# Chunk decays as running sums: a 4-row matmul and an identity matmul spread them, ScalarE's bias subtracts, and VectorE takes GpSimd's elementwise work

## The chip, the cores and the metric

The kernel runs on one core of one Trainium2 chip. The time is the device time of a whole launch in microseconds (us). A core has five instruction streams that work side by side and meet at semaphores: TensorE (PE, matmuls, results into PSUM), VectorE (DVE, elementwise), ScalarE (ACT, `exp`, `ln`, copies with scale and bias), GpSimd (POOL, elementwise from and to SBUF) and SyncE (SP, which issues most DMAs). Each works through its own instructions in the order in which they were laid down. An instruction at the head of a stream that waits holds back everything behind it there, whatever that is for.

## The reference

One encoder layer over 1,280 tokens (one sequence of 1,024, one of 256), 1,024 wide, in fp32: a projection into many columns, three mixers side by side (gated delta rule, retention, windowed attention), an output projection, a gated second input and a final norm. The change touches the gated delta rule's preparation, for chunks of 64 tokens, 6 heads and two directions:

```python
decay = jnp.cumsum(to_chunks(g, CHUNK), axis=-1)
incl = idx[:, None] >= idx[None, :]
gamma = jnp.exp(jnp.where(incl, decay[..., :, None] - decay[..., None, :], -jnp.inf))
a_mat = jnp.einsum('nbhcd,nbhsd->nbhcs', k_beta, k) * gamma
qk    = jnp.einsum('nbhcd,nbhsd->nbhcs', q, k) * gamma
q_dec = q * jnp.exp(decay)[..., None]
k_dec = k * jnp.exp(decay[..., -1:] - decay)[..., None]
```

`gamma` is a 64 x 64 matrix for each chunk and head: `exp` of the difference of two running sums of the gate `g` on one side of the diagonal, zero on the other. `t_mat`, the unit lower triangle of `a_mat`, is then inverted.

## The kernel before, in words

**Products.** Activations and weights are split in two fp32r parts (`xh`, `xl`; `whi`, `wlo`), and a product is a sum of three matmuls (`dense`, tile `mm`; two PSUM buffers of each tag). `load_w` fetches 128 columns of weights by SP, makes `whi` on ACT and `wlo` = raw - whi on POOL. In the gate products ACT evacuates (`evg`, tile `sz`, one buffer), three more ACT operations make the sigmoid in `sg`, POOL multiplies the two, and SP writes the result to DRAM.

**Convolutions.** Nine products feed a 5-tap convolution: four `scalar_tensor_tensor` of 128 x 1284 each on DVE (L522). Six of the nine (queries and keys) are normalised: ACT makes `rr`, POOL multiplies into `kq` (L544).

**Preparation** (`prep_stream`). It runs over ten blocks b of 128 tokens, from 9 down to 0, and in each over the two directions d, so 20 steps; PE's instructions of 11 products (`PP`) are spread between them. A step: DVE forms `gt` (128 x 768), the gates `ghl` (two fp32r parts) times a 0/1 triangle `MR`; two PE matmuls with `LA`, of which the one half sums and the other masks, turn it into decay differences in two PSUM tiles `sb`; ACT takes four `exp` of 64 x 384 into `ge` (L597); DVE multiplies `ge[:, 0]` by the triangle again to zero what lies beyond the diagonal (tile `ge`, L600). Then DVE multiplies Gram matrices (`sa`, in PSUM) and keys (`kc`) by `ge` into `at` and `l2`, POOL multiplies queries by `ge[:, 1]` into the rest of `l2` (L613), and SP writes `at` and `l2` to DRAM (`agd`, `ad`, `l2d`).

**Inversion** (`invert(g)`, group g=1 after block 5, g=0 after block 0). It reads `agd` back into `ot` and does some sixty dependent DVE operations of 120 rows; the result goes out as `yd`. The scan of the chunks (`join`, `step`) reads `yd` and runs beside attention and retention; the output projection follows.

**What sets the order.** `weave` and `spread` lay the work of the streams down by planned lengths, and the scheduler orders each engine's instructions from a simulated timeline; on the chip that order is fixed. Pool buffers decide how far one engine may run ahead of another: `sb`, `sa`, `tr` and `mm` have two PSUM buffers, `ge` and `l2` two, `gt`, `kc`, `at` and `sz` one.

Of the kernel before, what the change touches and what calls it, by code (L numbers as in the profile page):

```python
# [52 lines left out]
def encoder_kernel(ctx: ExitStack, tc: tile.TileContext, I, O, dbg=None, upto=99):  # L53
# [33 lines left out]
    def tt(eng, out, a, b, op):  # L87
        eng.tensor_tensor(out=out, in0=a, in1=b, op=op)  # L88
# [161 lines left out]
    for i in range(2):  # L250
        S.copy(LA[:, :, i, 64 - 64 * i:128 - 64 * i], bc(ones[:, 0:64].unsqueeze(1), [128, 2, 64]))
    for d in range(2):
        sg = 1 if d == 0 else -1
        t = tmpp.tile([128, 128], F32, name=f"mltmp{d}")
        sel(t, onesbd, ALU.is_gt, 0.0, 0, sg, [[-sg, 128]])
        tt(V, t[:, 0:64], t[:, 0:64], t[:, 64:128], ADD)
        for i in range(2):
            S.copy(LA[:, d, i, 64 * i:64 * i + 64], t[:, 0:64])
        t2 = pt_([128, 128], f"mrbd{d}")
        sel(t2, onesbd, ALU.is_ge, 0.0, 0, -sg, [[sg, 128]])  # L260
        MRbd.append(t2)
        m = pt_([128, 64], f"mr{d}")
        tt(V, m, t2[:, 0:64], t2[:, 64:128], ADD)
        MR.append(m)
# [201 lines left out]
    def product(n):  # L466
        if n in GCOL:
            def evg(pp, t0, w):
                o = ot[:, n, t0:t0 + w]
# [2 lines left out]
                S.copy(zt, pp[:, :w])  # L472
# [27 lines left out]
    with tc.tile_pool(name="pa", reuse_waits="tile", bufs=2) as pa:  # L500
# [65 lines left out]
        def prep_stream():  # L566
            for b in reversed(range(NB)):
# [18 lines left out]
                for d in range(2):  # L586
                    gt = pa.tile([128, 2, 6, 64], F32R, tag="gt", name=nm("gt"), bufs=1)
                    tt(V, gt, bc(ghl[:, d, :, 2 * b:2 * b + 2, :].bitcast(F32).rearrange("p l c q -> p l (c q)").unsqueeze(3),
                                 [128, 2, 6, 64]),
                       bc(MR[d].unsqueeze(1).unsqueeze(1), [128, 2, 6, 64]), MUL)  # L590
                    gf = [gt[:, i].rearrange("p q t -> p (q t)") for i in range(2)]
                    ge = pa.tile([128, 2, 2, 3, 64], F32, tag="ge", name=nm("ge"))
                    for i, r in enumerate((T, B)):
                        pd = ps("sb")
                        mm(pd[:, 0:384], LA[:, d, i], gf[i])
                        for w, rw in enumerate((T, B)):
                            S.activation(out=ge[rw, (w + i) % 2].rearrange("p c q t -> p (c q t)"), in_=pd[rw, 0:384], func=AF.Exp)  # L597
# [614 lines left out]
```

## Time and profile before

| what | us |
|---|---|
| median of 3 runs | 1153.72 |
| the runs | 1153.5 to 1154.53 |
| profiled execution | 1150.47 |
| its span (first to last instruction) | 1148.8 |

The mean granted TensorE clock over the span is 0.947 of full speed, and the DMA engines move 105 GB/s on average. In what follows a busy time is the time in which an engine had an instruction under way. A figure in square brackets behind a row of the timeline is how long the engine had been idle before it, and what ended that. A duration contains any time for which the instruction itself was held up after its start.

### The profile page before, as it was taken

The numbers are of one execution on the slowest core, as the hardware profiler recorded it, in microseconds if no ns is written. First come the engines' busy times: TensorE is split into PE (matmuls) and PEld (weight loads), VectorE is DVE, ScalarE is ACT, GpSimd is POOL, SyncE is SP. The second block draws the span as 40 slices with busy tenths as digits, with TensorE's granted clock in tenths as the row PEclk, the third lists the DMA queues.
The fourth block names the chain that finished last, engine by engine and source line by source line (L and its number), as shares of the span: only waits on it lengthen the run. The fifth ranks groups of instructions, "written<-read, shape, count | busy, mean of one in ns | idle before, by whom it ended". The sixth has DMA issues, their size and how long they took to land.

```text
span 1148.8 us, 25993 instructions
## 1 busy us (share of the span) xinstructions
PE 1042.9 (91%) x10345; PEld 959.0 (83%) x10345; DVE 666.8 (58%) x1297; ACT 531.3 (46%) x1208; POOL 426.2 (37%) x494
## 2 busy tenths in 40 slices
PE   6999989978778868799979999999879999999996
PEld 5989989968677867698868888888659999999996
DVE  6667667586899769626774465476856123411125
ACT  8575675666555433424643422323333012455554
POOL 3133333454554534114241434655462111214421
PEclk9999999999979888999988999999758999999998
DMA  7112202448244652435463343546547232101003
GB/s 243 37 43 60 61 19 60 117 144 195 74 126 136 164 136 84 87 77 134 123 148 92 96 116 104 140 116 168 148 138 240 90 102 92 46 2 47 10 37 147
DMA packets 196531, 120.63 MB, mean 105 GB/s; under 512 B 100266, under 2 KB 181338, under 8 KB 196410
## 3 DMA queue, kind: packets, MB, share of 16 engines
q1 hardware_dynamic: 196410, 118.97, 37.8%
q8 instruction: 82, 1.34, 0.5%
q14 instruction: 39, 0.32, 0.1%
HBM read 76.14 MB, written 42.78 MB: 104 GB/s over the span
## 4 chain that ended last, share of the span: by engine, by line
PE 58%; DVE 18%; DMA 9%; ACT 6%; issue 4%; SPq 3%; POOL 1%; DVEq 0%; ACTq 0%; POOLq 0%
PE mm L85 29%; PE sa L85 15%; DVE ot L88 8%; PE sb L85 7%; PE tr L85 3%; DVE ot L522 3%; DMA ad<-at 2%; SPq L616 1%; DMA agd<-at 1%; DVE l L88 1%; DMA ot<-agd 1%; PE tr L842 1%; DMA yd<-ot 1%; PE tr L1154 1%; ACT ge L597 1%
## 5 line engine op out<-in xcount | busy, mean ns | idle before, releaser
L85 PE MATMUL mm<-xh,whi 128*128 128x256 f32 x1200 | 351.5, 293 | 26.4 <-ACT sz L472 13.4
L85 PE MATMUL mm<-xl,whi 128*128 128x256 f32 x1200 | 348.2, 290 | 0.0
L85 PE MATMUL mm<-xh,wlo 128*128 128x256 f32 x1200 | 346.5, 289 | 0.2 <-POOL wlo L88 0.2
L85 PEld LDWEIGHTS mm<-xh,whi 128*128 128x128 f32 x1200 | 233.6, 195 | 34.3 <-ACT sz L472 15.2
L85 PEld LDWEIGHTS mm<-xl,whi 128*128 128x128 f32 x1200 | 233.4, 194 | 3.2 <-issue 1.4
L85 PEld LDWEIGHTS mm<-xh,wlo 128*128 128x128 f32 x1200 | 233.1, 194 | 3.4 <-issue 1.5
L88 POOL TENSOR_TENSOR wlo<-raw,whi 128x1024 fp32r<-128x1024 f32 (+1 forms) x37 | 106.7, 2885 | 207.7 <-ACT whi L1068 104.1
L88 DVE TENSOR_TENSOR ot<-ot 128x1284 f32<-128x1284 f32 (+16 forms) x131 | 115.8, 884 | 43.2 <-DMA ot<-agd 21.0
L85 PE MATMUL mm<-whi,xh 128*128 128x256 f32 x320 | 91.8, 287 | 0.0
L85 PE MATMUL mm<-whi,xl 128*128 128x256 f32 x320 | 91.7, 287 | 0.0
L85 PE MATMUL mm<-wlo,xh 128*128 128x256 f32 x320 | 91.7, 287 | 0.0
L85 PE MATMUL sa<-whi,xh 128*128 128x256 f32 x320 | 91.3, 285 | 0.1
L85 PE MATMUL sa<-whi,xl 128*128 128x256 f32 x320 | 90.8, 284 | 0.0
L85 PE MATMUL sa<-wlo,xh 128*128 128x256 f32 x320 | 90.5, 283 | 0.0
L522 DVE SCALAR_TENSOR_TENSOR ot<-ot,cols 128x1284 f32<-128x1284 f32 x36 | 76.1, 2115 | 23.1 <-ACT ot L517 22.3
L88 DVE TENSOR_TENSOR sgm<-sb,sgm 128x256 f32<-128x256 f32 x40 | 17.0, 424 | 94.7 <-ACT sgm L101 74.2
L88 POOL TENSOR_TENSOR l<-kq,ge 64x384 f32<-64x384 f32 x40 | 48.2, 1204 | 58.5 <-ACT ge L597 45.3
L88 POOL TENSOR_TENSOR ot<-ot,sgm 128x256 f32<-128x256 f32 x40 | 30.4, 761 | 88.9 <-DVE sgm L88 88.7
L85 PEld LDWEIGHTS mm<-whi,xh 128*128 128x128 f32 x320 | 61.8, 193 | 0.0
L85 PEld LDWEIGHTS mm<-whi,xl 128*128 128x128 f32 x320 | 61.6, 193 | 0.0
L85 PEld LDWEIGHTS mm<-wlo,xh 128*128 128x128 f32 x320 | 61.7, 193 | 0.0
L85 PEld LDWEIGHTS sa<-whi,xh 128*128 128x128 f32 x320 | 60.7, 190 | 0.4 <-DVE gt L1027 0.4
(289 smaller groups left out, 2217.2 us busy)
## 6 DMA issues: line engine op xcount, KB each, us to landing
raw<-in_w_in SPq DMA_DIRECT2D x28, 512.0 KB, 3.8
l2d<-l SPq DMA_DIRECT2D x20, 576.0 KB, 4.5
l<-l2d SPq DMA_DIRECT2D x40, 288.0 KB, 2.9
xt<-in_x_prompt SPq DMA_DIRECT2D x8, 512.0 KB, 6.6
x<-in_x_prompt SPq DMA_DIRECT2D x32, 128.0 KB, 2.3
raw<-in_w_pg SPq DMA_DIRECT2D x4, 1024.0 KB
yp<-ot SPq DMA_DIRECT2D x8, 512.0 KB, 2.6
ad<-at SPq DMA_DIRECT2D x20, 198.0 KB, 3.5
```

Of the source, the lines that this page charges most:

```text
L85: nc.tensor.matmul(out, lhsT, rhs, start=start, stop=stop)
L88: eng.tensor_tensor(out=out, in0=a, in1=b, op=op)
L522: V.scalar_tensor_tensor(out=Y[:, 0:1284], in0=R[:, j:j + 1284], scalar=cw(ti, j), in1=Y[:, 0:1284], op0=MUL, op1=ADD)
L597: S.activation(out=ge[rw, (w + i) % 2].rearrange("p c q t -> p (c q t)"), in_=pd[rw, 0:384], func=AF.Exp)
L616: nc.sync.dma_start(out=AGD[d][b // 5][q, 2 * b % 10:2 * b % 10 + 2].rearrange("c p r x -> r (c p) x"), in_=at[32 * q:32 * q + 32, :, :, q ...
L842: nc.tensor.transpose(pt[:, k * 128:(k + 1) * 128], pr[:, k * 128:(k + 1) * 128], ident)
L1154: nc.tensor.transpose(pt[:, k * 128:(k + 1) * 128], hb[:, b, (n * 4 + k) * 128:(n * 4 + k + 1) * 128], ident)
```

## The change

- **Decay.** A matmul `MRbd[d]` against the gates already made running sums (`pd`). Its negative is kept as `negd`. The running sums are also formed transposed (60 chunk-and-head rows), split in two fp32r parts (`dr`) and written to DRAM (`DRD`). Each step reads back four rows of 384 numbers into `dj` by two DMAs from POOL's queue. A matmul with four rows, `SD[i]` (0/1, which picks the half of the chunk pair), spreads them over the 128 partitions, and for i=0 an identity matmul adds a mask `MB` of 0 or -1e30. ACT takes six `exp` of 128 x 64 with `negd` as bias for `ge[:, 0]`, and one of 128 x 384 for `ge[:, 1]`. `gt`, `ghl`, `LA`, `MR` and the second masking are gone.
- **Engines.** `wlo` in `load_w`, the gate product in `evg`, the multiply into `kq` and the multiply of the queries into `l2` go from POOL to VectorE.
- **Buffers.** `sz` has two.

```diff
         with tc.high_priority():
             S.copy(hi, raw)
-            tt(G, lo, raw, hi.bitcast(F32), SUB)
+            tt(V, lo, raw, hi.bitcast(F32), SUB)
...
+    SD = [pt_([4, 128], f"sd{i}", F32R) for i in range(2)]
     for i in range(2):
+        for l in range(2):
+            for h in range(2):
+                nc.gpsimd.dma_start(out=SD[i][2 * l + h:2 * l + h + 1], in_=onesbd[64 * (h ^ i):64 * (h ^ i) + 1])
...
-        for d in range(2):
-            for i in range(2):
-                src = sab[64 * i:64 * i + 64, 1, d]
-                S.copy(ghl[0:64, d, i], src)
-                tt(V, ghl[64:128, d, i], src, ghl[0:64, d, i].bitcast(F32), SUB)
...
+            V.tensor_scalar(out=f(negd[:, d]), in0=pd[:, 0:60], scalar1=-1.0, scalar2=None, op0=MUL)
+            pr = ps("tr")
+            mm(pr[0:60, 0:128], f(sab[:, 1, d]), MRbd[d])
+            dr = pa.tile([60, 2, 128], F32R, tag="kc", name=nm("dr"), bufs=1)
+            S.copy(dr[:, 0], pr[0:60, 0:128])
+            tt(V, dr[:, 1], pr[0:60, 0:128], dr[:, 0].bitcast(F32), SUB)
+            nc.gpsimd.dma_start(out=DRD[d], in_=dr)
...
-                zt = gp.tile([128, 512], F32, tag="sz", name=nm("sz"), bufs=1)[:, :w]
+                zt = gp.tile([128, 512], F32, tag="sz", name=nm("sz"))[:, :w]
                 S.copy(zt, pp[:, :w])
                 sigmoid(sg, zt)
-                tt(G, sg, sg, zt, MUL)
+                tt(V, sg, sg, zt, MUL)
...
-                        tt(G, kq[:, p, 1 if isq else 0, t0 + s0:t0 + s0 + n], Z[:, o + s0:o + s0 + n], rr[:, :n], MUL)
+                        tt(V, kq[:, p, 1 if isq else 0, t0 + s0:t0 + s0 + n], Z[:, o + s0:o + s0 + n], rr[:, :n], MUL)
...
-                    gt = pa.tile([128, 2, 6, 64], F32R, tag="gt", name=nm("gt"), bufs=1)
-                    tt(V, gt, bc(ghl[:, d, :, 2 * b:2 * b + 2, :].bitcast(F32).rearrange("p l c q -> p l (c q)").unsqueeze(3),
-                                 [128, 2, 6, 64]),
-                       bc(MR[d].unsqueeze(1).unsqueeze(1), [128, 2, 6, 64]), MUL)
+                    dj = pa.tile([4, 6, 64], F32R, tag="dj", name=nm("dj"))
+                    for l in range(2):
+                        nc.gpsimd.dma_start(out=dj[2 * l:2 * l + 2], in_=DRD[d][6 * b:6 * b + 6, l].rearrange("n (s t) -> s n t", s=2))
...
-                    for i, r in enumerate((T, B)):
+                    for i in range(2):
                         pd = ps("sb")
-                        mm(pd[:, 0:384], LA[:, d, i], gf[i])
-                        for w, rw in enumerate((T, B)):
-                            S.activation(out=ge[rw, (w + i) % 2].rearrange("p c q t -> p (c q t)"), in_=pd[rw, 0:384], func=AF.Exp)
-                    gm = ge[:, 0].rearrange("p c q t -> p (c q) t")
-                    tt(G if b in MG else V, gm, gm, bc(MR[d].unsqueeze(1), [128, 6, 64]), MUL)
+                        mm(pd[:, 0:384], SD[i], djf, stop=bool(i))
+                        if i == 0:
+                            mm(pd[:, 0:384].rearrange("p (n t) -> p n t", n=6), identR, bc(MB[d].unsqueeze(1), [128, 6, 64]), start=False)
+                            for n in range(6):
+                                S.activation(out=ge[:, 0, n // 3, n % 3], in_=pd[:, 64 * n:64 * n + 64], func=AF.Exp,
+                                             bias=negd[:, d, 2 * b + n // 3, n % 3:n % 3 + 1])
+                        else:
+                            S.activation(out=ge[:, 1].rearrange("p c q t -> p (c q t)"), in_=pd[:, 0:384], func=AF.Exp)
...
-                        tt(G, l2[lr, :, :, h, :], kq[lr, :, 1, tb].rearrange("p q (c t) -> p c q t", c=2), ge[lr, 1], MUL)
+                        tt(V, l2[lr, :, :, h, :], kq[lr, :, 1, tb].rearrange("p q (c t) -> p c q t", c=2), ge[lr, 1], MUL)
```

VectorE's order at the start of the preparation, before (names: `ge`, `gt`, `at`, `l` are a step's tiles, `sa` the Gram matrices, `mr` the triangle, `kc` the keys; the number behind a name tells tiles apart):

```order
L88 TENSOR_TENSOR ge_2170<-ge_2170,mr_334 128x384
L88 TENSOR_TENSOR at_2180<-sa_2145,ge_2170 128x6x32
L88 TENSOR_TENSOR l_184_2181<-sa_2145,ge_2170 64x3x64 x2
L88 TENSOR_TENSOR at_2180<-sa_2152,ge_2170 128x6x32
L88 TENSOR_TENSOR l_184_2181<-sa_2152,ge_2170 64x3x64 x2
L88 TENSOR_TENSOR l_184_2181<-kc_2163,ge_2170 128x6x64
L88 TENSOR_TENSOR gt_2367<-ghl,mr_334 128x768
L88 TENSOR_TENSOR ge_2265<-ge_2265,mr_343 128x384
```

and the same place now:

```order
L88 TENSOR_TENSOR at_2193<-sa_2154,ge_2180 128x6x32
L88 TENSOR_TENSOR l_188_2194<-sa_2154,ge_2180 64x3x64 x2
L88 TENSOR_TENSOR at_2193<-sa_2161,ge_2180 128x6x32
L88 TENSOR_TENSOR l_188_2194<-sa_2161,ge_2180 64x3x64 x2
L88 TENSOR_TENSOR l_188_2194<-kc_2172,ge_2180 128x6x64
L88 TENSOR_TENSOR l_188_2194<-kq,ge_2180 64x6x64 x2
L88 TENSOR_TENSOR wlo_2708<-raw_2705,whi_2707 128x1024
L88 TENSOR_TENSOR at_2292<-sa_2154,ge_2279 128x6x32
```

A step has lost its two triangle multiplies, and POOL's two multiplies of queries and its weight split stand in VectorE's stream.

VectorE's order where the first inversion begins, before (`ot<-ot` rows are the inversion, the first of them waits for `agd` to come back):

```order
L88 TENSOR_TENSOR l_283_3032<-kc_2891,ge_3021 128x6x64
L88 TENSOR_TENSOR ot<-ot 120x2x32x32
L88 TENSOR_TENSOR ot<-ot 120x2x30 x2
L88 TENSOR_TENSOR ot<-ot 120x2x58
L88 TENSOR_TENSOR ot<-ot 120x2x2x29
```

and now (`sg<-sg,sz` are gate products, `wlo` the weights of a product to come):

```order
L88 TENSOR_TENSOR sg_3255<-sg_3255,sz_3256 128x512
L88 TENSOR_TENSOR ot<-ot 120x2x32x32
L88 TENSOR_TENSOR ot<-ot 120x2x30 x2
L88 TENSOR_TENSOR ot<-ot 120x2x58
L88 TENSOR_TENSOR ot<-ot 120x2x2x29
L88 TENSOR_TENSOR ot<-ot 120x2x84
L88 TENSOR_TENSOR ot<-ot 120x2x3x28
L88 TENSOR_TENSOR ot<-ot 120x2x108
L88 TENSOR_TENSOR sg_3330<-sg_3330,sz_3331 128x512
L88 TENSOR_TENSOR ot<-ot 120x2x4x27
L88 TENSOR_TENSOR wlo_3392<-raw_3389,whi_3391 128x1024
```

Gate products and weight splits now stand between and behind the inversion's operations, behind the one that waits for a DMA.

POOL's order in the preparation now (`dj` the four decay rows of a step, `drd` their place in DRAM, `elc` a small copy that stays on POOL):

```order
L373 DMA drd_382<-dr_924 60x256
L594 DMA dj_2276<-drd_382 2x6x64 x2
L594 DMA dj_2384<-drd_381 2x6x64 x2
L525 MEMSET ot 128x4 x5
L621 COPY elc<-ge_2180 128x6
L594 DMA dj_2501<-drd_382 2x6x64 x2
L621 COPY elc<-ge_2279 128x6
```

The `dj` loads of a step stand two steps ahead of the copy that belongs to it.

More of the change, by code (lines that the diff above doesn't have):

```diff
@@ L244, in sel @@
                         pattern=pat, channel_multiplier=cm)
-    MR, MRbd = [], []
-    LA = pt_([128, 2, 2, 128], "la", F32R)
-    for i in range(2):
-        S.copy(LA[:, :, i, 64 - 64 * i:128 - 64 * i], bc(ones[:, 0:64].unsqueeze(1), [128, 2, 64]))
-    for d in range(2):
[L253 to L256, printed above, removed]
-        for i in range(2):
[L258 to L264, printed above, removed]
+    identR = pt_([128, 128], "identR", F32R)
+    S.copy(identR, ident)
+    MRbd, MB = [], []
+    for d in range(2):
+        t2 = ot[:, 7, 256 + 128 * d:384 + 128 * d]
+        sel(t2, onesbd, ALU.is_ge, 0.0, 0, 2 * d - 1, [[1 - 2 * d, 128]])
+        MRbd.append(t2)
+        t = tmpp.tile([128, 64], F32, name=f"mbtmp{d}")
+        tt(V, t, t2[:, 0:64], t2[:, 64:128], ADD)
+        m = pt_([128, 64], f"mb{d}", F32R)
+        V.tensor_scalar(out=m, in0=t, scalar1=-1.0, scalar2=1e30, op0=ADD, op1=MUL)
+        MB.append(m)
+    SD = [pt_([4, 128], f"sd{i}", F32R) for i in range(2)]
+    for i in range(2):
+        for l in range(2):
+            for h in range(2):
+                nc.gpsimd.dma_start(out=SD[i][2 * l + h:2 * l + h + 1], in_=onesbd[64 * (h ^ i):64 * (h ^ i) + 1])
     sumid = pt_([128, 24], "sumid")
@@ L310, in encoder_kernel @@
     sab = ct([128, 2, 2, NC, 3], "sab")
-    ghl = ct([128, 2, 2, NC, 3], "ghl", F32R)
+    negd = ct([128, 2, NC, 3], "negd")
     nbeta = ct([128, 2, NC, 3], "nbeta")
@@ L314, in encoder_kernel, with beta_alpha @@
     elc = ct([128, 2, NC, 3], "elc")
-    def beta_alpha():
+    DRD = [tc.dram_tile([60, 2, 128], F32R, name=f"drd{d}") for d in range(2)]
+    def beta_alpha(pa):
         abT = ot[:, 6, 0:NT]
@@ L355, in beta_alpha @@
                         (V if f else G).tensor_copy(dst[:, f, d, :, par, :], src[:, f, :, d, :, 1 - half])
-        for d in range(2):
-            for i in range(2):
-                src = sab[64 * i:64 * i + 64, 1, d]
-                S.copy(ghl[0:64, d, i], src)
-                tt(V, ghl[64:128, d, i], src, ghl[0:64, d, i].bitcast(F32), SUB)
         V.tensor_scalar(out=nbeta, in0=sab[:, 0], scalar1=-1.0, scalar2=None, op0=MUL)
@@ L509, in encoder_kernel @@
             if i == 2:
-                beta_alpha()
+                beta_alpha(pa)
             R, Y, Z = ot[:, 3 * z, :], ot[:, 3 * z + 1, :], ot[:, 3 * z + 2, :]
@@ L586, in prep_stream @@
                 for d in range(2):
-                    gt = pa.tile([128, 2, 6, 64], F32R, tag="gt", name=nm("gt"), bufs=1)
-                    tt(V, gt, bc(ghl[:, d, :, 2 * b:2 * b + 2, :].bitcast(F32).rearrange("p l c q -> p l (c q)").unsqueeze(3),
-                                 [128, 2, 6, 64]),
-                       bc(MR[d].unsqueeze(1).unsqueeze(1), [128, 2, 6, 64]), MUL)
-                    gf = [gt[:, i].rearrange("p q t -> p (q t)") for i in range(2)]
+                    dj = pa.tile([4, 6, 64], F32R, tag="dj", name=nm("dj"))
+                    for l in range(2):
+                        nc.gpsimd.dma_start(out=dj[2 * l:2 * l + 2], in_=DRD[d][6 * b:6 * b + 6, l].rearrange("n (s t) -> s n t", s=2))
+                    djf = dj.rearrange("r n t -> r (n t)")
                     ge = pa.tile([128, 2, 2, 3, 64], F32, tag="ge", name=nm("ge"))
-                    for i, r in enumerate((T, B)):
+                    for i in range(2):
                         pd = ps("sb")
-                        mm(pd[:, 0:384], LA[:, d, i], gf[i])
-                        for w, rw in enumerate((T, B)):
-                            S.activation(out=ge[rw, (w + i) % 2].rearrange("p c q t -> p (c q t)"), in_=pd[rw, 0:384], func=AF.Exp)
-                    gm = ge[:, 0].rearrange("p c q t -> p (c q) t")
-                    tt(G if b in MG else V, gm, gm, bc(MR[d].unsqueeze(1), [128, 6, 64]), MUL)
+                        mm(pd[:, 0:384], SD[i], djf, stop=bool(i))
[6 more added lines that the diff above has]
+                            S.activation(out=ge[:, 1].rearrange("p c q t -> p (c q t)"), in_=pd[:, 0:384], func=AF.Exp)
                     at = pa.tile([128, 2, 3, 2, 33], F32, tag="at", name=nm("at"), bufs=AB)
@@ L610, in prep_stream @@
                         tt(V, l2[B, r, :, 0, :], g3[r][B, :, 64:128], ge[B, 0, r], MUL)
-                    tt(G if b in KG else V, l2[:, :, :, 2, :], kc, bc(gl, [128, 2, 3, 64]), MUL)
+                    tt(V, l2[:, :, :, 2, :], kc, bc(gl, [128, 2, 3, 64]), MUL)
                     for h, lr in enumerate((T, B)):
-                        tt(G, l2[lr, :, :, h, :], kq[lr, :, 1, tb].rearrange("p q (c t) -> p c q t", c=2), ge[lr, 1], MUL)
+                        tt(V, l2[lr, :, :, h, :], kq[lr, :, 1, tb].rearrange("p q (c t) -> p c q t", c=2), ge[lr, 1], MUL)
                     G.tensor_copy(elc[:, d, 2 * b:2 * b + 2, :], el.rearrange("p c q t -> p c (q t)"))
```

## Prediction

> **What bounds the kernel now.** I read the page's busy table first, then busy time by stage, then the waits, then the timeline around the longest waits.
>
> ```profile
> PE 1042.9 (91%) x10345; PEld 959.0 (83%) x10345; DVE 666.8 (58%) x1297; ACT 531.3 (46%) x1208; POOL 426.2 (37%) x494
> core 0: us, PE busy (x) PEld busy (x) DVE busy (x) ACT busy (x) POOL busy (x), PEclk, DMA share, GB/s
> 9.00:40.00 31.00, 28.10 (x201) 26.15 (x200) 24.51 (x32) 25.26 (x61) 5.13 (x2) 1.00 0.51 163
> 40.00:219.00 179.00, 172.36 (x1418) 160.43 (x1417) 114.46 (x105) 116.06 (x192) 61.48 (x45) 0.99 0.22 53
> 219.00:279.00 60.00, 49.73 (x417) 45.56 (x416) 52.68 (x89) 40.15 (x88) 37.90 (x37) 0.97 0.57 155
> 279.00:320.00 41.00, 28.30 (x238) 27.07 (x237) 29.01 (x32) 18.11 (x34) 16.03 (x12) 0.91 0.39 99
> 320.00:396.00 76.00, 62.52 (x487) 59.29 (x487) 69.12 (x119) 43.06 (x94) 39.77 (x37) 0.87 0.55 148
> 396.00:485.00 89.00, 68.07 (x614) 64.40 (x613) 68.00 (x130) 31.68 (x68) 30.29 (x36) 0.89 0.45 108
> 485.00:640.00 155.00, 148.30 (x2228) 127.37 (x2229) 85.31 (x270) 65.67 (x177) 49.51 (x67) 0.94 0.46 112
> ```
>
> The columns are the stretch, its length, the busy time of PE, PEld, DVE, ACT and POOL, the granted clock, DMA. PE is the bound of the whole, but unevenly: 96% in the convolutions (40 to 219) and 96% after 485. From 219 to 485, preparation and both inversions, it is busy 49.73 + 28.30 + 62.52 + 68.07 = 208.6 of 266 us: 57 us idle, of 106 in the whole span. In 219 to 279 and 320 to 396 DVE is the busiest engine, 88% and 91%. This **stage of 266 us** is what the change can shorten; behind it PE has work in hand, so what is saved here should come out at the end.
>
> What does PE wait for there?
>
> ```profile
> L85 PE MATMUL sb<-gt,la 128*128 128x384 f32 x40 | 14.0, 398 | 25.2 <-DVE gt L88 18.5 <-ACT sg L100 4.6 <-ACT ge L597 2.1
> PE mm L85 <- ACT sz L472: 13.4, 6, 9.6
> ACT sz L472 <- POOL sg L88: 21.3, 7, 9.8
> 290.46 9.55 DVE L88 TENSOR_TENSOR ot<-ot 120x2048 f32<-120x2048 f32 x7 [11.02 <-DMA ot<-agd]
> 318.13 0.95 DVE L88 TENSOR_TENSOR gt<-ghl,mr 128x768 fp32r<-128x768 f32 x1
> 319.23 0.66 PE L85 MATMUL sb<-gt,la 128*128 128x384 f32 x1 [10.71 <-DVE gt L88]
> 414.15 9.41 DVE L88 TENSOR_TENSOR ot<-ot 120x2048 f32<-120x2048 f32 x5 [9.95 <-DMA ot<-agd]
> 418.03 1.84 POOL L88 TENSOR_TENSOR yc<-yn,mblk 128x960 f32<-128x960 f32 x1 [11.64 <-DMA yn<-yd]
> 422.13 1.29 POOL L88 TENSOR_TENSOR sg<-sg,sz 128x512 f32<-128x512 f32 x1
> 423.88 0.58 PE L85 MATMUL mm<-xh,whi 128*128 128x256 f32 x1 [9.64 <-ACT sz L472]
> ```
>
> 25.2 us are before the decay matmul, which needs `gt` from DVE; the longest, 10.71, is DVE coming to `gt` at 318 only after half an inversion. 13.4 us are before products whose PSUM buffer ACT has not evacuated, since `sz` (one buffer) waits for POOL's gate product; the longest, 9.64, is POOL standing at `yc` for a DMA with the gate product behind it. Together 38.6 of the 57 us.
>
> **DVE and POOL hold each other up.**
>
> ```profile
> L88 DVE TENSOR_TENSOR ge<-ge,mr x20: 543/590/5048, 218.6 to 393.8; 128x384 f32<-128x384 f32 x20
> L88 DVE TENSOR_TENSOR at<-sa,ge x40: 357/358/363, 219.2 to 395.4; 128x192 f32<-128x192 f32 x40
> L88 DVE TENSOR_TENSOR l<-kc,ge x20: 559/560/2554, 221.2 to 396.4; 128x384 f32<-128x384 f32 x20
> L88 DVE TENSOR_TENSOR ot<-ot x131: 222/617/4949, 54.9 to 473.1; 128x1284 f32<-128x1284 f32 x9, 120x60 f32<-120x60 f32 x8, 120x116 f32<-120x116 f32 x8, 120x168 f32<-120x168 f32 x8
> L522 DVE SCALAR_TENSOR_TENSOR ot<-ot,cols x36: 1543/1556/3592, 41.9 to 199.1; 128x1284 f32<-128x1284 f32 x36
> ```
>
> These give min/median/max of one shape in ns. The triangle multiply has the same shape twenty times and takes 543 to 5048 ns, the convolution 1543 to 3592. These operations have both inputs in SBUF; multiplies with one input in PSUM (`at<-sa,ge`) do not spread. I read the excess over the median as time blocked by POOL, and expect it back where POOL falls silent.
>
> **The change part by part, on DVE in the 266 us.**
>
> ```profile
> L88 DVE TENSOR_TENSOR gt<-ghl,mr 128x768 fp32r<-128x768 f32 x20 | 25.9, 1297 | 2.0 <-PE sb L85 1.9
> L88 DVE TENSOR_TENSOR ge<-ge,mr 128x384 f32<-128x384 f32 x20 | 20.1, 1004 | 12.8 <-ACT ge L597 12.8
> L88 DVE TENSOR_TENSOR l<-kc,ge 128x384 f32<-128x384 f32 x20 | 19.6, 982 | 0.8 <-ACT kc L585 0.2
> L88 DVE TENSOR_TENSOR ot<-ot 128x1284 f32<-128x1284 f32 (+16 forms) x131 | 115.8, 884 | 43.2 <-DMA ot<-agd 21.0 <-ACT ot L101 19.4
> L88 DVE TENSOR_TENSOR ot<-ot 128x1284 f32<-128x1284 f32 x9 | 15.1, 1676 | 19.4 <-ACT ot L101 19.4
> L88 DVE TENSOR_TENSOR sq<-ot,sq 128x512 fp32r<-128x512 f32 x12 | 7.8, 683 | 1.1 <-ACT sq L535 1.1
> L88 DVE TENSOR_TENSOR sq<-ot,sq 128x256 fp32r<-128x256 f32 x6 | 2.5, 422 | 6.5 <-ACT sq L535 6.5
> L88 POOL TENSOR_TENSOR l<-kq,ge 64x384 f32<-64x384 f32 x40 | 48.2, 1204 | 58.5 <-ACT ge L597 45.3 <-issue 11.7
> ```
>
> - Removed: `gt` 25.9 and the second masking 20.1, so -46.0.
> - Contention returned: `l<-kc` 20 x (982 - 560) = -8.4; the inversions are 131 - 9 operations of 115.8 - 15.1 = 100.7 us, 825 ns each against a median of 617, so 122 x 0.21 = -25.
> - Added: 40 multiplies of queries, 64 x 384. The nearest DVE row, two SBUF inputs of 384, has a median of 0.56 to 0.59: +23. Gate products: 16 of 512 and 8 of 256 elements, priced by `sq`, 16 x 0.683 + 8 x 0.422 = +14.3. Weight splits of 1024: `sq` grows by (683 - 422)/256 = 1.02 ns an element, so 683 + 512 x 1.02 = 1.2 us; some twelve in this stage, +14.5.
> - DVE was busy 52.68 + 29.01 + 69.12 + 68.00 = 218.8; now 218.8 - 46.0 - 33.4 + 51.8 = 191.
>
> DVE's two waits for `ot<-agd` (11.02 + 9.95 = 21) stay, because they hang on at, DMA out, DMA back. With them DVE filled 218.8 + 21 = 240 of 266 and left 26 us of slack; now it needs 212. If 10 to 26 us of slack stay, the stage lasts 222 to 238, a gain of 28 to 44.
>
> The same from PE's side: the 25.2 us before the decay matmul go, because `dj` needs no DVE and is loaded two steps ahead; so do the 13.4 at `sz`, which gets a second buffer and is freed by DVE. Late next are `ge`'s two buffers, freed by DVE's multiplies, and the Gram banks. Against it stand new matmuls:
>
> ```profile
> 890.63 2.88 PE sa L85 x24
> L597 ACT ACTIVATE ge<-sb 64x384 f32<-64x384 f32 x80 | 38.9, 486 | 14.6 <-PE sb L85 12.9 <-DMA vtd<-vt 0.4
> L894 ACT ACTIVATE wt<-dp,lgb 128x128 f32<-128x128 f32 x12 | 4.0, 392 | 0.8 <-DVE wret L898 0.8
> L1014 ACT ACTIVATE sab<-sab 128x6 f32<-128x6 f32 x10 | 2.1, 206 | 0.2
> ```
>
> In the chain 24 matmuls of 256 columns follow each other in 2.88 us, 0.12 each, so 0.18 for 384. A step has three instead of two: 20 x 0.18 = +3.6. So 38.6 - 3.6 = 35, in the middle of DVE's 28 to 44. **I take -35.**
>
> - ACT: four `exp` of 486 ns (1.94 us) become six of 128 x 64 with a bias and one of 128 x 384 (0.49). One of the six lies between 206 (6 elements) and 392 (128 elements, a scale from memory): 1.73 to 2.84 a step, so -4 to +18 us over 20 steps. ACT is busy 133 of 266; that idle time hides it. Without that cover it would be the +18.
> - `dj`: no row shows a DMA from POOL's queue. Hidden it costs 0, which I take; fully exposed it is priced under the rivals.
> - Opening (9 to 40): DVE is busy 24.51 of 31 between norms and splits, PE waits for it, and two weight splits join: between 0 and 2 x 1.2; I take +1.
> - Convolutions: DVE gains 36 x (2.115 - 1.556) = -20 (76.1 us in the L522 group, mean 2115), and takes nine weight splits (11) and eighteen multiplies into `kq`, by `sq` 12 x 0.683 + 6 x 0.422 (10.7): about 116 of 179, as now. PE, at 96%, hides it: 0, within -5 to +5. The small start-up work (SD, MB, dr) lies here too.
> - After 485: eight weight splits, 10 us on a DVE busy 55% up to 640, while POOL loses theirs: 0.
>
> ```profile
> L522 DVE SCALAR_TENSOR_TENSOR ot<-ot,cols 128x1284 f32<-128x1284 f32 x36 | 76.1, 2115 | 23.1 <-ACT ot L517 22.3
> ```
>
> **Sum:** -35 + 1 + 0 + 0 = -34. The profiled execution took 1150.47 (span 1148.8 and 1.7 around it), 3.25 below the median of 1153.72. 1150.47 - 34 = 1116.5; on the scale of the median 1153.7 - 34 = **1120**. With the bounds of slack and ACT, 1108 to 1132.
>
> **Rivals.**
>
> *DVE's queue takes over the waits (1140).* Everything POOL did now stands in line with the inversions. At `ot<-agd` DVE stands still for 11.02 and 9.95 us with gate products and weight splits behind it, and PE can go on for two `mm` banks and two `sz` buffers. For it: the 9.64 us above was just that on POOL. Against it: a gate product is placed ahead of each inversion, and PE's order leaves it 216 product matmuls at 0.12 (26 us) before it runs out of banks. If both waits reach PE, 21 us come back: 1120 + 21, about 1140.
>
> *The clock comes back too (1101).* The granted clock is 0.91, 0.87 and 0.89 in the stretches from 279 on, 0.97 before, where PE's waits are short. Lost clock is 60 x 0.03 + 41 x 0.09 + 76 x 0.13 + 89 x 0.11 = 25 us, of which PE was busy 208.6/266, so 20. With it PE needs 208.6 - 20 + 3.6 = 192 and DVE's 212 becomes the bound: 266 - 212 = 54, less 1: 1153.7 - 53 = 1101. [...]
>
> *Late decay rows (slower, 1178).* `dj` goes to DRAM and back by POOL's queue, in which it stands behind `elc`, which waits for ACT.
>
> ```profile
> agd<-at SPq DMA_DIRECT2D x80, 24.8 KB, 2.9
> ```
>
> The nearest small DRAM transfer lands 2.9 us after its issue. If each step shows that to PE, 20 x 2.9 = 58: 1120 + 58 = 1178. It decides from 34/20 = 1.7 us a step on. Against it: a load may start when the step two before has used its buffer, and two steps now last 2 x 222/20 = 22 us. [...]
>
> **Chances.** Forecast 0.55, DVE's queue 0.22, clock 0.15, late rows 0.08. Of the 0.22 I give 0.18 to faster by over 0.2% (about what a measurement of this kernel can tell from no change), 0.03 to within, 0.01 to slower. Faster 0.55 + 0.15 + 0.18 = 0.88, same 0.03, slower 0.09. For 8 in 10 the range reaches from the clock case to beyond the queue case: 1100 to 1146.
>
> **What would show it.** Right: no `gt`; `l<-kc`, `ot<-ot` and the convolution near their medians; PE idle before `sb` and before `mm <- ACT sz` below 10 us together; the stage from the first `at` to the end of the second inversion about 35 us shorter, and the rest of equal length. Wrong: PE waiting for `dj`; DVE idle at `ot<-agd` while PE waits at `sz` or `wlo`; a convolution stage longer than 184 us; or an earlier end of the stage that later waits swallow.

## The result and the profile after

The changed kernel took **1114.58 us** (median of 4 runs, 1111.01 to 1119.53) beside 1153.61 for the kernel before (4 runs): a ratio of **0.9668**, 95% interval 0.9625 to 0.9711. Run again beside the variants below it had 0.9689 (0.9665 to 0.9713). The forecast was 1120, with a range of 1100 to 1146. The profiled execution took 1116.26, its span is 1114.6. One launch of the variant `sz_one` (5331.59 us) and one of the kernel before (1178.19 us) fell into a slower state and stand outside the ratios below.

The busy row of the page after:

```profile
PE 1059.6 (95%) x10369; PEld 963.9 (86%) x10369; DVE 638.1 (57%) x1369; ACT 522.3 (47%) x1261; POOL 268.8 (24%) x430
```

PE's idle time has gone from 106 to 55 us. To see where, I cut both spans at the same four events: the first convolution operation on DVE, the first `at`, the end of the second inversion (its last MEMSET), the end. Busy time by stage (columns as in the prediction), before and then after:

```profile
0.00:41.90 41.90, 30.75 (x219) 28.83 (x220) 27.31 (x41) 32.43 (x78) 9.24 (x39) 1.00 0.55 179
41.90:219.20 177.30, 170.66 (x1404) 158.73 (x1403) 114.64 (x105) 114.56 (x189) 61.08 (x45) 0.99 0.22 53
219.20:473.50 254.30, 202.09 (x1707) 191.99 (x1706) 212.62 (x342) 125.68 (x263) 122.20 (x114) 0.91 0.49 128
473.50:1148.80 675.30, 639.45 (x7020) 579.45 (x7020) 312.24 (x810) 258.65 (x679) 233.72 (x298) 0.95 0.38 105
```

```profile
0.00:44.50 44.50, 31.27 (x223) 29.63 (x224) 29.62 (x44) 31.74 (x73) 7.18 (x42) 1.00 0.53 169
44.50:214.20 169.70, 169.07 (x1404) 157.59 (x1403) 108.69 (x131) 112.96 (x187) 8.20 (x23) 1.00 0.24 55
214.20:440.10 225.90, 210.71 (x1729) 191.56 (x1728) 180.32 (x381) 119.06 (x323) 34.39 (x74) 0.95 0.56 147
440.10:1114.60 674.50, 648.57 (x7018) 585.09 (x7018) 319.50 (x817) 258.55 (x679) 219.02 (x291) 0.93 0.38 105
```

The differences are opening +2.6, convolutions -7.6, stage -28.4, rest -0.8: -34.2 in all. In the stage PE's idle time fell from 52.2 to 15.2 (-37.0) and its busy time rose by 8.6. What PE still waits for most, from the view of waits (total, times, longest; the first row is the start of the program):

```profile
PE tr L219 <- DVE mb L257: 8.0, 1, 8.0
PE mm L85 <- ACT ot L392: 5.6, 1, 5.6
PE sa L85 <- DVE sv L88: 3.5, 3, 1.6
PE mm L85 <- DVE kst L88: 2.4, 2, 1.4
PE sa L85 <- DVE l L88: 2.4, 1, 2.4
```

The timeline around the longest wait of the stage:

```profile
365.93 0.11 DVE L426 MEMSET ot<- 120x64 f32 x1
...
366.08 1.07 ACT L392 COPY ot<-mm 128x512 f32<-128x512 f32 x2 [3.51 <-DVE ot L426]
...
366.72 0.58 PE L85 MATMUL mm<-xh,whi 128*128 128x256 f32 x1 [5.59 <-ACT ot L392]
```

The waits at `gt` and `sz` are gone from this list. The longest that is left is new: the product `cv` is copied into row 1 of `ot`, and that copy waits for the last operation of the first inversion, which works in rows 0 and 3. DVE's groups, first the convolution from the whole span, then those of the stage alone:

```profile
L527 DVE SCALAR_TENSOR_TENSOR ot<-ot,cols 128x1284 f32<-128x1284 f32 x36 | 55.9, 1552 | 0.5
```

```profile
L88 DVE TENSOR_TENSOR ot<-ot 120x60 f32<-120x60 f32 (+15 forms) x122 | 70.9, 581 | 10.7 <-DMA ot<-agd 7.6
...
L88 DVE TENSOR_TENSOR l<-kq,ge 64x384 f32<-64x384 f32 x40 | 22.0, 550 | 0.7 <-ACT ge L606 0.2
...
L88 DVE TENSOR_TENSOR wlo<-raw,whi 128x1024 fp32r<-128x1024 f32 x11 | 13.4, 1220 | 7.2 <-ACT whi L148 7.1
L88 DVE TENSOR_TENSOR l<-kc,ge 128x384 f32<-128x384 f32 x20 | 11.2, 558 | 0.5
L88 DVE TENSOR_TENSOR sg<-sg,sz 128x512 f32<-128x512 f32 (+1 forms) x18 | 10.7, 597 | 4.4 <-ACT sg L101 4.3
L88 DVE TENSOR_TENSOR ot<-ot,sz 128x512 f32<-128x512 f32 (+1 forms) x6 | 3.6, 601 | 4.3 <-ACT ot L101 4.3
```

Every operation that was spread is back near its median. Last, the decay's own rows, of the tiles `dj` and `ge` (min/median/max in ns, and the time from a load's issue to its landing):

```profile
L594 POOL DMA_DIRECT2D dj<-drd x40: 546/546/595, 95.5 to 347.8; - x40
...
DMA to landing us min/median/max: 1.7/3.2/6.2
```

```profile
L603 ACT ACTIVATE ge<-sb,negd x120: 297/322/362, 213.4 to 361.8; 128x64 f32<-128x64 f32 x120
L606 ACT ACTIVATE ge<-sb x20: 472/524/543, 214.6 to 362.0; 128x384 f32<-128x384 f32 x20
```

### The profile page after: what moved, and what is told of

Its sections match the earlier page's. It is cut to its first block, busy times and chain, and to the rows that moved or that the text cites. A ratio compares the mean times of both kernels' runs of the same rounds, so it can differ in the third digit from the quotient of the medians.

```text
span 1114.6 us, 26117 instructions
## 1 busy us (share of the span) xinstructions
PE 1059.6 (95%) x10369; PEld 963.9 (86%) x10369; DVE 638.1 (57%) x1369; ACT 522.3 (47%) x1261; POOL 268.8 (24%) x430
## 4 chain that ended last, share of the span: by engine, by line
PE 51%; DVE 7%; DMA 3%; POOL 2%; issue 2%; ACT 1%; SPq 0%; POOLq 0%; DVEq 0%; ACTq 0%
PE mm L85 22%; PE sa L85 15%; PE sb L85 7%; PE tr L85 3%; DVE ot L88 2%; PE tr L849 1%; POOL oo L88 1%; PE tr L1161 1%; DMA an<-ad 1%; DVE ot L967 1%; DMA yn<-yd 1%; PE tr L948 1%; DMA vt<-vtd 1%; DMA oo<-od 1%; PE sa L1033 1%
## 5 line engine op out<-in xcount | busy, mean ns | idle before, releaser
L85 PEld LDWEIGHTS mm<-xh,whi 128*128 128x128 f32 x1200 | 232.2, 194 | 15.4 <-ACT ot L392 5.8
L85 PEld LDWEIGHTS mm<-xl,whi 128*128 128x128 f32 x1200 | 232.2, 194 | 4.7 <-issue 2.8
L88 DVE TENSOR_TENSOR ot<-ot 128x1284 f32<-128x1284 f32 (+16 forms) x131 | 84.3, 644 | 20.6 <-ACT ot L101 9.9
L85 PEld LDWEIGHTS sa<-whi,xl 128*128 128x128 f32 x320 | 60.2, 188 | 0.0
L85 PEld LDWEIGHTS sa<-wlo,xh 128*128 128x128 f32 x320 | 60.1, 188 | 0.0
L88 POOL TENSOR_TENSOR wlo<-raw,whi 128x2048 fp32r<-128x2048 f32 x7 | 33.2, 4744 | 102.2 <-ACT whi L1075 99.0
L85 PE MATMUL sa<-sv,l 128*64 128x64 f32 (+1 forms) x912 | 49.9, 242 | 7.9 <-DVE sv L88 3.5
```

The lines of the kernel that those rows point to most:

```text
L85: nc.tensor.matmul(out, lhsT, rhs, start=start, stop=stop)
```

## The experiments

All ratios are to the kernel before on the same chip, and the lengths are cut at the same four events in one profiled execution each.

| kernel | ratio (95%) | opening | conv. | stage | rest |
|---|---|---|---|---|---|
| before, two profiles | 1 | 41.9, 42.2 | 177.3, 177.7 | 254.3, 252.7 | 675.3, 674.4 |
| changed, first | 0.9668 (0.9625-0.9711) | 44.5 | 169.7 | 225.9 | 674.5 |
| after_again | 0.9689 (0.9665-0.9713) | 44.6 | 169.8 | 220.0 | 673.2 |
| decay_only | 0.9897 (0.9863-0.9931) | 44.0 | 170.1 | 237.6 | 683.3 |
| moves_only | 0.9779 (0.9745-0.9813) | 42.3 | 168.8 | 232.2 | 679.7 |
| queries_pool | 0.9728 (0.9685-0.9771) | 44.2 | 169.7 | 227.9 | 668.3 |
| wlo_pool | 0.9779 (0.9727-0.9830) | 44.0 | 168.5 | 236.3 | 673.3 |
| sz_one | 0.9761 (0.9738-0.9784) | 44.5 | 169.8 | 231.9 | 672.3 |
| triangle_kept | 0.9728 (0.9711-0.9744) | 44.6 | 171.9 | 224.1 | 670.9 |
| mask_three | 0.9778 (0.9754-0.9803) | 46.4 | 169.7 | 236.5 | 667.8 |
| open_pool | 0.9666 (0.9648-0.9684) | 44.6 | 169.7 | 218.9 | 672.5 |
| mask_rows | 0.9717 (0.9694-0.9740) | 44.9 | 168.8 | 220.6 | 676.5 |
| rows_cv | 0.9745 (0.9719-0.9771) | 47.1 | 168.7 | 225.5 | 672.6 |

0.001 is 1.15 us. Each edit also makes the scheduler lay the instructions down in another order, so a difference of 2 or 3 us is not put down to an edit; the stages of the two profiles of the changed kernel lie 5.9 us apart with no edit at all. In `decay_only` that order puts some 200 of PE's matmuls behind the stage (7260 there, 7020 before), so only the sum of its last two columns compares with the other rows.

### The two halves apart

`decay_only` is the changed kernel with GpSimd's work given back and `sz` with one buffer; `moves_only` is the kernel before with the four operations moved:

```diff
 decay_only, against the changed kernel
-            tt(V, lo, raw, hi.bitcast(F32), SUB)
+            tt(G, lo, raw, hi.bitcast(F32), SUB)
...
 moves_only, against the kernel before
-            tt(G, lo, raw, hi.bitcast(F32), SUB)
+            tt(V, lo, raw, hi.bitcast(F32), SUB)
-                tt(G, sg, sg, zt, MUL)
+                tt(V, sg, sg, zt, MUL)
...
```

(and the same for `sg`, `kq` and the queries in `l2`).

> The kernel before with the new decay alone: GpSimd keeps the weight splits, gate products, the multiplies into kq and the multiplies of queries, sz has one buffer. Theory one, parts add by their waits: the 25.2 us before the decay matmul go, 9 us of new matmul time come, the 13.4 us at sz, the spread of VectorE's operations and the convolutions stay as before: about 1154 - 25 + 9 = 1138. Theory two, the decay rework is nearly the whole gain, since it alone takes 46 us from VectorE: 1120 or less. Theory three, GpSimd's queue takes the place of the wait (dj loads and gate products stand behind yc there): above 1146.

> The kernel before with the moves alone: weight splits, gate products, kq and query multiplies on VectorE, the old decay with gt and the triangle, sz with one buffer (there is no room for two beside gt). Theory one, parts add by their waits: 7.6 us in the convolutions and some 10 us at sz are won, 2.6 us lost in the opening: about 1154 - 15 = 1139. Theory two, VectorE's queue: it gets 52 us and wins back 33 from the spread, so gt comes 19 us later than before and the convolutions' 7.6 us are all that is won: 1150 to 1166. The duration of l<-kc near 0.56 us and of the convolution operation near 1.55 us is expected under both.

`decay_only` is 1136.55 against 1149.18, -12.6: near theory one's -16. `moves_only` is 1123.27, **-25.9**, more than either theory allowed. The two sum to -3.24%, and the whole change gave -3.11 to -3.32%. That is no sign that the halves add up: neither has the second buffer of `sz`, which the change has. Both halves with one buffer are `sz_one`, further down: -2.39%. They overlap by some 0.85%, 10 us, and the buffer, for which the decay rework makes the room, makes up for nearly that much. The waits of PE, `decay_only` and then `moves_only`:

```profile
PE mm L85 <- ACT sz L477: 19.4, 4, 13.7
...
PE sb L85 <- ACT ge L603: 7.0, 4, 3.7
```

```profile
PE mm L85 <- ACT ot L387: 24.0, 2, 21.6
PE mm L85 <- ACT sz L472: 13.6, 6, 5.7
```

With the decay alone the gate products' buffer is the wait. With the moves alone it is the end of the first inversion, 21.6 us at once, and `gt` is in neither list: in `moves_only` PE's one wait for it in the stage was 0.68 us. `gt` is still made there, but DVE comes to it in time; that its shorter work is the reason is argued from these rows (before, the two groups had 25.9 and 20.1 us):

```profile
L88 DVE TENSOR_TENSOR gt<-ghl,mr 128x768 fp32r<-128x768 f32 x20 | 19.0, 951 | 0.1
...
L88 DVE TENSOR_TENSOR ge<-ge,mr 128x384 f32<-128x384 f32 x20 | 10.9, 546 | 0.1
```

The stage of `moves_only` (columns as above) shows that PE's waits were mostly shifted there, not removed: 38.7 of 232.2 us are idle, against 52.2 before, at the granted clock of before, 0.91.

```profile
211.10:443.30 232.20, 193.54 (x1698) 185.67 (x1696) 203.80 (x416) 124.86 (x262) 19.97 (x39) 0.91 0.51 140
```

### GpSimd's work given back in part

`queries_pool` gives back only the 40 multiplies of queries, `wlo_pool` only the weight splits:

```diff
 queries_pool
-                        tt(V, l2[lr, :, :, h, :], kq[lr, :, 1, tb].rearrange("p q (c t) -> p c q t", c=2), ge[lr, 1], MUL)
+                        tt(G, l2[lr, :, :, h, :], kq[lr, :, 1, tb].rearrange("p q (c t) -> p c q t", c=2), ge[lr, 1], MUL)
 wlo_pool
-            tt(V, lo, raw, hi.bitcast(F32), SUB)
+            tt(G, lo, raw, hi.bitcast(F32), SUB)
```

> The changed kernel with the 40 multiplies of queries back on GpSimd. If GpSimd's elementwise work is what spread VectorE's durations, l<-kc and the inversion's operations in the preparation get longer again (mean of l<-kc above 0.8 us against 0.558), while the convolution operation stays at 1.55 us; VectorE has slack, so the time moves by 0 to +8 us against the changed kernel (1115 to 1123). If the spread came from gt or the triangle instead, l<-kc stays at 0.56 us and the time at 1115 or a few us below, since VectorE has 22 us less to do.

> The changed kernel with all weight splits of load_w back on GpSimd. Theory one, the convolutions won 7.6 us because GpSimd no longer slows VectorE: the convolution operation is spread again (mean above 1.75 us against 1.55), PE idles again in the convolutions, the opening wins its 2.6 us back; in sum 1115 + 2 to + 8. Theory two, the convolutions won for another reason (the multiply into kq no longer waits in GpSimd's queue): they stay at about 170 us, and with the opening the time is 2 to 3 us below the changed kernel. A third way: a weight split stands in GpSimd's queue behind an operation that waits for a DMA, PE waits for wlo, and the time is more than 8 us above.

DVE's groups, the first row of `queries_pool`, and then two of `wlo_pool`:

```profile
L88 DVE TENSOR_TENSOR l<-kc,ge 128x384 f32<-128x384 f32 x20 | 14.8, 742 | 0.5
```

```profile
L527 DVE SCALAR_TENSOR_TENSOR ot<-ot,cols 128x1284 f32<-128x1284 f32 x36 | 70.0, 1943 | 15.4 <-ACT ot L522 14.8
...
L88 DVE TENSOR_TENSOR l<-kc,ge 128x384 f32<-128x384 f32 x20 | 15.4, 769 | 0.4
```

The spread comes back with either (742 and 769 ns for `l<-kc`, 558 in the changed kernel), so GpSimd's elementwise work beside it is its cause; the 0.8 us expected of `queries_pool` was a little too much. Its ratio is 0.004 to 0.006 above the changed kernel's, 4 to 7 us, with intervals that overlap. `wlo_pool` had a result that no theory had. The convolution operation is spread again, 1943 ns, and yet the convolutions take 168.5 us; in `decay_only`, with `kq` on GpSimd too, the operation takes 2012 ns and the convolutions 170.1 us. **Their 7.6 us are not a matter of contention.** The loss, some 10 us, is in the stage: DVE gave away 13.4 us of splits and was busy 191.0 us instead of 180.3; I estimate 191.0 - 180.3 + 13.4 = 24 us of contention from that.

### Both kernels profiled again

> The changed kernel again, beside the three below on one chip: a ratio of 0.963 to 0.971 to the kernel before. If the shorter convolutions and the 5.6 us wait at the end of the preparation are the kernel's own and not one execution's, both are in this profile too: 168 to 171 us from the first convolution operation to the first at, and one wait of mm for ACT's copy into ot, which waits for the end of the first inversion, of 4 to 8 us.

> The kernel before, profiled a second time. The four variants so far have 168 to 172 us from the first convolution operation to the first at, whichever engines they use, and the one profile of before has 177. If the convolutions of before are really longer, this profile shows 175 to 179 with PE idle for 5 to 8 us there; if it was that one execution, 169 to 172.

Both repeat: the wait is 5.7 us, and the convolutions of before take 177.7 us with the same seven waits of PE (the longest 1.5 us). So the 7.6 us are no matter of one execution. All ten variants have 168 to 172 us, with the splits and `kq` on either engine, and what they share is that the instructions were laid down in another order than before. That the order is the cause is concluded by elimination, not shown; which step of it was not tried. The second profile of the changed kernel has a stage of 220.0 us, 5.9 less than the first, with the same work: its granted clock there is 0.98, against 0.95. By the prediction's estimate, the length times the missing share of the clock, that is 220.0 x 0.02 = 4.4 us of clock lost, against 225.9 x 0.05 = 11.3, a difference of 6.9.

### The second buffer of sz

```diff
-                zt = gp.tile([128, 512], F32, tag="sz", name=nm("sz"))[:, :w]
+                zt = gp.tile([128, 512], F32, tag="sz", name=nm("sz"), bufs=1)[:, :w]
```

> The changed kernel with one buffer of sz. Theory one, sz is freed soon enough now that VectorE multiplies the gates: no wait of PE behind sz above 1 us, 0 to +2 us. Theory two, the gate product stands in VectorE's stream behind the inversion and the multiplies of a step, as in the variant with the moves alone (13.6 us of waits at sz): 8 to 14 us of such waits, the time +4 to +12 us.

The ratio is 0.9761 against 0.9689: **+8 us**. The timeline of `sz_one` where the second inversion begins:

```profile
384.14 3.81 DVE L88 TENSOR_TENSOR ot<-ot 120x2048 f32<-120x2048 f32 x1 [12.74 <-DMA ot<-agd]
387.88 2.28 DVE L88 TENSOR_TENSOR sg<-sg,sz 128x512 f32<-128x512 f32 x1
...
390.89 0.58 PE L85 MATMUL mm<-xh,whi 128*128 128x256 f32 x1 [7.36 <-ACT sz L477]
```

DVE stands 12.74 us for `agd` with the gate product behind it, and PE waits 7.36 us for the buffer. That is the rival of the prediction in which DVE's queue takes over the waits; the second buffer is what keeps it away (PE's waits in `after_again` have none at `sz`). Beside `moves_only` (0.9779, also one buffer) `sz_one` (0.9761) shows that the decay rework adds 2 us to the moves as long as `sz` has one buffer, less than the intervals can tell from nothing. So the decay rework pays, beside the moves, mostly by the room that it makes; that the buffer had none beside `gt` is the author's count, and no run has both. The decay rework with two buffers and without the moves was not tried. The two stages are 232.2 and 231.9 us long, though PE is idle for 38.7 us in the one and for 22.8 in the other, and DVE busy for 203.8 and 182.4: the stage's length goes by neither figure alone.

### What the stage hangs on

`triangle_kept` puts an operation where the second masking was, `mask_three` lays the mask's matmul down three times:

```diff
 triangle_kept
+                    gm = ge[:, 0].rearrange("p c q t -> p (c q) t")
+                    tt(V, gm, gm, bc(MB[d].bitcast(F32).unsqueeze(1), [128, 6, 64]), ALU.max)
 mask_three: identity matmul x3, the first two with stop=False
```

> The changed kernel with VectorE's second masking kept as a maximum of ge and the mask, which changes no value: 20 operations of 128 x 384 more on VectorE, 11 us. Theory one, the decay rework pays because it takes work from VectorE, whose first inversion must end before PE may go on: of the 11 us at least 8 come back at the wait for the end of the first inversion (5.6 us now, 13 to 17 then), the time is 8 to 12 us above the changed kernel. Theory two, VectorE has slack (180 of 226 us busy): 0 to 3 us above.

> The changed kernel with the identity matmul of the mask laid down three times a step, 40 matmuls more (the mask's values become three times as negative, ge is the same). Theory one, a matmul of 384 columns costs PE 0.18 us, as the prediction had it: +7 us. Theory two, it costs the 0.44 us of its row, since PE's stage is 93 per cent busy: +15 to +18. Theory three, PE is not what the stage hangs on, but VectorE's first inversion: 0 to +3, and the 5.6 us wait shrinks.

`mask_rows` takes 20 matmuls out by putting the mask into rows 0 to 63 of the tile whose rows 64 to 67 are the decay rows, with two identities in the matching rows of `SD`; `rows_cv` is that with another order of products:

```diff
 mask_rows
-                    dj = pa.tile([4, 6, 64], F32R, tag="dj", name=nm("dj"))
+                    dj = DJ[d]
...
-                        mm(pd[:, 0:384], SD[i], djf, stop=bool(i))
+                        mm(pd[:, 0:384], SD[i], djf)
...
-                            mm(pd[:, 0:384].rearrange("p (n t) -> p n t", n=6), identR, bc(MB[d].unsqueeze(1), [128, 6, 64]), start=False)
 rows_cv, besides
-PP = ["cq0", "cq1", 6, 7, 3, 4, 0, 5, "cv", 1, 2]
+PP = ["cq0", "cq1", "cv", 6, 7, 3, 4, 0, 5, 1, 2]
```

> The changed kernel with the mask and the four decay rows in one tile of 68 rows, so that one matmul spreads the rows and adds the mask: 20 matmuls less, the same ge. Theory one, a matmul of 384 columns costs 0.27 us here, as 40 more of them cost 10.8 us: 5 us below the changed kernel (ratio about 0.964). Theory two, without these matmuls PE only waits longer for the end of the first inversion: the 5.7 us wait grows by the same amount and the time is unchanged.

> The variant with the mask and the decay rows in one tile, and the product cv, whose copy into row 1 of ot had to wait for the end of the first inversion (rows 0 and 3 of ot), moved from ninth to third place among the eleven products, ahead of that inversion. Theory one, that copy is all that PE waits for there, and PE is the bound behind it: the 11.6 us wait goes, the stage gets 8 to 12 us shorter than in the variant it is made from (220.6), the ratio to the kernel before is 0.960 to 0.965. Theory two, VectorE's stream is the bound of the stage: the wait goes, but PE waits as long at the second inversion's end or behind sz, the stage keeps 218 to 223 us and the ratio 0.970 to 0.973.

The longest wait of PE in the stage, in `triangle_kept`, in `mask_rows` and in `rows_cv` (L813 is a transposition that reads `ot` when the second inversion is done):

```profile
PE mm L85 <- ACT ot L392: 14.8, 2, 14.1
```

```profile
PE mm L85 <- ACT ot L392: 11.6, 1, 11.6
```

```profile
PE tr L813 <- DVE ot L88: 17.2, 1, 17.2
```

- `triangle_kept`: 11.1 us of DVE work lengthen the wait by 8.4 us, as theory one had it, but the time only by 5 us (1116.47 against 1111.15): between the theories. Its stage, 224.1 us, lies between the two profiles of the changed kernel (220.0 and 225.9).
- `mask_three`: +10.8 us for 40 matmuls (0.0089 of 1148 is 10, 6 to 14 by the intervals), 0.16 to 0.35 us each. Neither 0.18 is excluded nor 0.44 reached. The wait at the first inversion's end did not shrink, as theory three had it; it grew from 5.7 to 8.4 us, and DVE's own idle time before `at`, until ACT's `exp`, to 16.8 (4.2 and 11.8 in the two profiles of the changed kernel). That suggests that the added matmuls held up DVE as well.
- `mask_rows`: theory two. 20 matmuls less, a wait longer by 5.9 us, the end of the second inversion at 434.3 us instead of 434.4, no gain. The first inversion ended 1.8 us earlier, and DVE then stood 10.76 us before the second, against 6.91 in `after_again`.
- `rows_cv`: theory two again, a little beyond its figures. The 11.6 us are gone, and 17.2 us stand at the end of the second inversion. The stage is not shorter (225.5).

So work added on PE or on DVE costs time, and 20 matmuls taken from PE gain none. How the stage ends is in the view of the chain that ended last, in `after_again` (start, length, what; three of its pieces):

```profile
361.29 9.77 DMA yd<-ot
...
371.15 6.78 DMA ot<-agd
...
378.01 4.16 DVE ot L88
```

The first inversion's result leaves `ot`, then `agd` comes into it, and from 378 on nearly every piece up to the end of the stage is DVE's, at the second inversion and what stands between its operations. In the first profile of the changed kernel other DMAs stand ahead of the inversion (`an` 8.32 us, `yn` 2.10). Further ahead no one engine has the chain: over the whole stage of `mask_rows`, PE's `mm`, `sa` and `sb` matmuls are 38% of it, the inversions 16%. So the stage ends with **the second inversion and the DMAs ahead of it**; its first part passes between PE, ACT and DVE. What taking work from the inversion would gain was not tried.

### The opening

```diff
+            nw[0] += 1
-            tt(V, lo, raw, hi.bitcast(F32), SUB)
+            tt(G if nw[0] <= 2 else V, lo, raw, hi.bitcast(F32), SUB)
```

> The changed kernel with the first two weight splits, those of the opening, on GpSimd as before. Theory one, they cost the opening its 2.6 us, since VectorE is what PE waits for there: the first convolution operation starts at 42 instead of 44.5, and the time is 2 to 3 us below the changed kernel. Theory two, the opening got longer by the small start-up work that stands in VectorE's and GpSimd's streams (PE waited 8.0 us for the mask mb, at the very start): no change, the first convolution operation at 44.

The first convolution operation starts at 44.6, as in the changed kernel: theory two for the opening. `moves_only`, with the splits on DVE, has 42.3, `decay_only` 44.0. So the opening's loss came with the decay rework, its start-up work or the order laid down with it, and not with the splits. In the order one exchange is seen on ACT at the second block's norm, before and then after (`ln`, `exp`, copy of `xh`):

```profile
8.98 0.29 ACT L213 ACTIVATE ssx<-ssx,cols 128x1 f32<-128x1 f32 x1
9.31 0.20 ACT L214 ACTIVATE ssx<-ssx 128x1 f32<-128x1 f32 x1
...
10.46 0.56 ACT L227 CAST xh<-tr 128x512 fp32r<-128x512 f32 x1
```

```profile
8.98 0.29 ACT L213 ACTIVATE ssx<-ssx,cols 128x1 f32<-128x1 f32 x1
9.18 0.57 ACT L227 CAST xh<-tr 128x512 fp32r<-128x512 f32 x1
9.64 0.20 ACT L214 ACTIVATE ssx<-ssx 128x1 f32<-128x1 f32 x1
```

That this alone makes the 2.6 us was not tried. The time of `open_pool`, 1108.1, is the lowest median here, but its interval overlaps that of the changed kernel and the opening it was meant for is unchanged, so it is not claimed to be better.

## Why the prediction was right, and where it was wrong

The total was right: -34 forecast, -34.2 in the first profile, -39.4 between the second ones, -39.0 between the medians. The terms were not all right; two errors cancelled (the stage gained less, the convolutions more), and that the total fits as well as this is luck.

- **The waits (38.6 us): right in size.** 0.4 us of them is left. The reason given was too narrow: the 25.2 us were to go "because `dj` needs no DVE", but `moves_only` has only 0.7 us of them with `gt` in place. There, though, 21.6 us stand at the end of the first inversion and 13.6 at `sz`: the moves alone shift the waits. PE's idle time falls to 15.2 us only with the decay rework and the second buffer.
- **DVE's terms: right.** Queries 22.0 (23 forecast), gate products 10.7 + 3.6 = 14.3 (14.3), weight splits 13.4 (14.5), `l<-kc` -8.4 (-8.4), inversions 100.7 to 70.9, -29.8 (-25; it was worked out from the median of a group of 17 shapes, so that it came near is in part luck). Forecast for the same cut: 191 less the 6.0 of 473.5 to 485, 185; measured 180.3.
- **DVE's slack: wrong in kind.** The two `ot<-agd` waits were to stay at 21 us; they are 7.6 (7.8 in the second profile). And DVE was treated as a sum (191 + 21 = 212) to be compared with PE's, with slack to spare. It binds as part of a chain: with 45 us idle in the stage, its second inversion still sets the end.
- **What is late next: wrong.** `ge`'s buffers and the Gram banks were named; they cost 0.4 and 2.4 us. PE's wait for the end of the first inversion, 5.6 us, was not thought of.
- **New matmuls (+3.6): not settled.** PE's busy time rose by 8.6 in the first pair of profiles and by 5.9 in the second (200.0 to 205.9), but a busy time contains what an instruction is held up (on DVE the same `l<-kc` took 982 ns before and 558 after). By time, the 0.16 to 0.35 us each of `mask_three` make 3.2 to 7 for 20, and `mask_rows` gained nothing by leaving 20 out.
- **The stage (-35): -28.4 and -32.7.** The forecast lies beyond both by 2 to 7 us. The waits that were not thought of are of that size, but that they make the difference is argued; and by the estimate above the changed kernel's first profile lost some 7 us more clock in the stage than its second.
- **The convolutions (0, within 5): wrong, -7.6 and -7.9.** The step that failed is that PE's 96% there leaves nothing to gain: PE's 6.6 us of waits all but vanished (0.6). That contention on DVE is hidden there was right: in `wlo_pool` and `decay_only` the operation takes 1943 and 2012 ns and the convolutions 168.5 and 170.1 us.
- **The opening (+1, 0 to 2.4): +2.6,** and not by the splits that were priced.
- **ACT: right.** A step's `exp` take 6 x 0.322 + 0.524 = 2.46 us, within 1.73 to 2.84, and PE waits 0.4 us for them. DVE waits 11.8 us for them before `at` (4.2 in the second profile), about the 12.8 us of before at the triangle. After the stage: -0.8 (0).

The rivals:

- **DVE's queue.** The mechanism exists (7.36 us in `sz_one`), and the change brought the buffer that covers it.
- **The clock.** It did come back in the stage, in part: 0.91 before, 0.95 and 0.98 after. By the same estimate the stage lost 254.3 x 0.09 = 23 us of clock before and 225.9 x 0.05 = 11 after, and 4.4 in the second profile. But the stage got 28 and 33 us shorter, not the rival's 54, and in `moves_only` it is 22 us shorter at an unchanged 0.91, so most of its gain does not need the clock; what the rest of it owes to the clock, no run separates. Behind the stage the lost clock rose from 675.3 x 0.05 = 34 to 674.5 x 0.07 = 47 us, and that part was no longer for it.
- **Late decay rows.** No wait of PE for `dj` is in the list; the slowest load landed after 6.2 us. The lead is shorter than the 22 us forecast, since the 20 steps lie between 213.4 and 362 us: two steps are some 15 us. In `queries_pool` PE did wait for `dj` once, 1.3 us. What DVE's operations do to such loads, no run separates: with DVE busy for 80% of the stage (180.3 of 225.9 us), they landed 1.7 to 6.2 us after their issue.

## What to carry to other kernels

When one engine's durations spread over a factor of two to nine at one shape, price what the rival engine does beside it before pricing the engine's own work. Here the convolution took 1543 to 3592 ns and the triangle multiply 543 to 5048: moving GpSimd's elementwise operations to VectorE made VectorE less busy, not more (212.6 us of the stage before, 203.8 in `moves_only`), and alone gave two thirds of the gain. Ask of freed memory what buffer it allows, since a second buffer of 2 KB a partition was worth about 8 us here, and ask of a saving which chain ends next: the 20 matmuls that `mask_rows` saves gained nothing. Two halves measured apart say what the whole owes to each only if the whole holds nothing else. A total that comes out right says little of its terms; cut both spans at the same events and compare each piece.
